# A boundary's instructions put in another order, and a last LayerNorm whose shift is summed by TensorE

## The chip, the cores and the metric

The kernel runs on one core of one Trainium2 chip. The core has five engines with queues of their own: TensorE (PE in the profile; PEld is its weight loads), VectorE (DVE), ScalarE (ACT), GpSimd (POOL) and SyncE (SP, which issues the transfers here). Each works through its queue in order, and semaphores tie the queues together. Data lie in HBM, in the SBUF (128 partitions) and in the PSUM, into which TensorE writes (8 banks of 512 fp32 per partition). The metric is the device time of one execution in microseconds.

## What is computed

One inference step of a two-layer decoder for a prompt of 256 tokens and for 8 samples of 4 tokens with the same weights, width 1024, all in fp32. Layer 0 mixes with a gated linear attention (GLA), layer 1 with dilated window attention over a shared key and value store. Each layer is FFN, mixer, FFN, and after each of these six sub-layers there is a LayerNorm:

```python
def modulate(x, shift, scale):
    return x * (1.0 + scale[:, None, :]) + shift[:, None, :]

def post_norm(x, y, gate, g, b):
    return layer_norm(ALPHA * x + (1.0 + gate[:, None, :]) * y, g, b)
...
        y = swiglu(modulate(x, sh1, sc1), p['w_ffn1_up'][l], p['w_ffn1_down'][l])
        x = post_norm(x, FFN_RES * y, g1, p['ln_g'][l, 0], p['ln_b'][l, 0])
        h = modulate(x, sh2, sc2)
        ...
        x = post_norm(x, y, g2, p['ln_g'][l, 1], p['ln_b'][l, 1])
        y = swiglu(modulate(x, sh3, sc3), p['w_ffn2_up'][l], p['w_ffn2_down'][l])
        x = post_norm(x, FFN_RES * y, g3, p['ln_g'][l, 2], p['ln_b'][l, 2])
```

The shifts, scales and gates come from products of a conditioning vector with `w_ada` (nine per layer, two more for keys and values).

## The kernel before, in words

**Layout.** All 288 tokens (256 of the prompt, 32 of the samples) stand in the free dimension, the width in 8 chunks of 128 partitions. `z` and `ax` hold the LayerNorm's input and the scaled residual, `xh` and `xl` the next sub-layer's input.

**Three products for one.** Each fp32 number is split into a high half, rounded to a faster type (fp32r), and a low half, the rest. `mm3` (from L529) makes high x high (L531), high weight x low input (L532) and low weight x high input (L533). The input's halves are xh and xl, the weight's are made by `split_part` (from L173): the high half by ScalarE (L177), the low half by VectorE (L179), a piece of 128 x 1024 at a time.

**The weight stream.** `Stream` loads all weights as one list of jobs (`job_list`), cut into pieces, through 11 raw buffers. A job is a weight ("w", split into one of 4 buffers for either half), raw data ("r"), or a step of the conditioning products ("ada": 16 TensorE matmuls for each, L450). `take` hands out the next weight and splits the one after it ahead; `more(n)` splits n more pieces; `fill` does the ada jobs that are next in the list. `weave` mixes two lists of jobs.

**Order.** The kernel's instructions are put in queue order by a list scheduler: by its own estimate of time, an engine that is free takes what is ready, first what the program wrote first. `pin(chain, ...)` makes an instruction follow the last one of the same chain ("act", "dve", "pe"). What is not pinned may be put into any gap that the scheduler sees.

**A boundary.** The LayerNorm between two sub-layers is prepared while the last products run (`Post.chunk`, `Post.stats`) and ended in `post_norm` (L771 to 801): `spread` brings 1/deviation to all partitions (L651), then for each of the 8 chunks VectorE subtracts the mean (`center`, L668), scales (L758, and for the samples L763 and L764), ScalarE rounds to xh (L760, L765), and VectorE makes xl (L767, L769). The xl of a chunk is issued after the first steps of the next chunk. At the third chunk one more weight piece is split (`S.more(1)`), both halves. All this is pinned. TensorE meanwhile begins the next sub-layer with `project_chunkwise`: the first two weights' four outputs, chunk by chunk (L549 and L551 for the first chunk, then L531 to L533).

**The residual.** `Post.residual` (from L670) forms ALPHA times the LayerNorm's output for the sub-layer after: per chunk one VectorE product (L676) and one addition of the bias on GpSimd (L678). It is a generator that yields after every second chunk. Its instructions are not pinned. The FFN draws it in its loop over the hidden dimension, two chunks per step; the GLA mixer draws all of it ahead of the keys' projection; the dilated mixer draws all of it after its first four outputs, ahead of their rotations. There are five boundaries, and so 40 of each of these two instructions.

**GLA and dilated mixer.** In the loop over `("wv", i)` (from L1159) the GLA mixer projects the values and between the projections prepares its decay levels on VectorE (`level`, four products and more for each level) and takes their products on TensorE. The dilated mixer rotates each projected query (`rotate`, L1288 to 1298): four copies by ScalarE (L1294), two products by VectorE (L1295) and GpSimd (L1296), a sum by VectorE (L1298). Its outputs stand in the four "pa" banks of the PSUM until L1294 and L1295 have read them.

**The last LayerNorm.** `Final` transposes each finished chunk of the sum back to tokens in partitions (L700, L701), takes statistics (L704, L707), multiplies by the gain (L711), and after the last chunk `finish` makes the output in six units (three token tiles, two halves of the width): a shift, gain x (-mean/deviation) + bias, and then y x (1/deviation) + shift (L736), which is stored (L738). Three units form the shift on VectorE (L730), three by ScalarE (L733) and GpSimd (L734):

```python
                if x in ON_DVE:
                    V.scalar_tensor_tensor(out=v, in0=gr[0:n, f], scalar=self.r[0:n, 1, t:t + 1], in1=br[0:n, f],
                                           op0=ALU.mult, op1=ALU.add)
                else:
                    A.mul(v, gr[0:n, f], self.r[0:n, 1, t:t + 1])
                    G.tensor_tensor(out=v, in0=v, in1=br[0:n, f], op=ALU.add)
                yv = self.y[0:n, t, f]
                V.scalar_tensor_tensor(out=yv, in0=yv, scalar=self.r[0:n, 0, t:t + 1], in1=v, op0=ALU.mult, op1=ALU.add)
```

## Time and profile before

| | |
|---|---|
| median of 3 runs | 1561.36 us (1559.15 to 1568.56) |
| the profiled execution | 1566.59 us |
| its span (first to last instruction) | 1564.5 us |
| TensorE busy | 1487.1 us, 95% |
| VectorE busy | 927.6 us, 59% |
| ScalarE busy | 715.7 us, 46% |
| GpSimd busy | 217.2 us, 14% |
| read from HBM | 332.36 MB, 218 GB/s over the span |

Times in the rows below are in microseconds from the span's start unless they are marked ns. A row of a timeline has the start, the duration, the engine, the line in the kernel, the operation, what it writes and reads, the sizes, how many such instructions were merged, and in brackets how long the engine had been idle and who ended that. Successive instructions overlap a little in such rows, so the distance between two starts tells more than a duration. A busy TensorE need not be at its full pace: a matmul that waits for its input can look busy.

### The profile page before, as it was taken

To read this page: it belongs to the slowest core of one execution; us is meant where nothing else is said; L and a number is where in the kernel's file an instruction comes from. 1 tells how busy PE (TensorE), PEld (TensorE's weight loads), DVE (VectorE), ACT (ScalarE), POOL (GpSimd) and SP (SyncE) were. 2 spreads that over 40 slices of the span, in tenths; PEclk is the share of its full clock that TensorE was granted. 3 is DMA by queue.
4 is the path that set the end of the run, shared out by engine and by line. 5 is a ranking of instruction groups with operands and counts; after the bars stand their busy time and mean duration, and the time that the engine had idled before them with its cause. 6 is when DMAs were issued, how large, how long until landed. Compare 5 with 4: busy or idle time off the path is not lost.

```text
span 1564.5 us, 31623 instructions
## 1 busy us (share of the span) xinstructions
PE 1487.1 (95%) x12706; PEld 1336.2 (85%) x12706; DVE 927.6 (59%) x2020; ACT 715.7 (46%) x1178; POOL 217.2 (14%) x312
## 2 busy tenths in 40 slices
PE   6999999999899999998999999999999989899996
PEld 4999998799778999998899999898766638899995
DVE  3644545596786444448745444675775667755455
ACT  2443434755744444346444433486543343444432
POOL 0000031201522000224100003232301002200001
PEclk8999999999999999999999999999998989999998
DMA  9977685636856767864566676767687997555520
GB/s 300 321 228 241 213 273 160 214 99 199 293 190 217 233 216 236 299 209 152 179 206 204 202 239 204 250 195 246 226 303 278 348 329 256 193 162 162 175 82 31
DMA packets 238420, 342.67 MB, mean 219 GB/s; under 512 B 12471, under 2 KB 201985, under 8 KB 238274
## 3 DMA queue, kind: packets, MB, share of 16 engines
q1 hardware_dynamic: 235810, 333.34, 64.7%
q0 software_dynamic: 2048, 7.14, 1.2%
q8 instruction: 99, 1.62, 0.4%
q14 instruction: 47, 0.39, 0.1%
q10 hardware_dynamic: 416, 0.17, 0.0%
HBM read 332.36 MB, written 8.26 MB: 218 GB/s over the span
## 4 chain that ended last, share of the span: by engine, by line
PE 83%; DVE 9%; ACT 3%; issue 2%; DMA 1%; POOL 0%; SPq 0%; DVEq 0%; ACTq 0%; POOLq 0%
PE pa L531 21%; PE pa L532 21%; PE pa L533 21%; PE pd L450 4%; PE pb L1381 4%; PE pa L1384 3%; PE pa L1381 2%; DVE lo L179 1%; PE pa L1042 1%; ACT pe L1407 1%; DVE xm L758 1%; DVE ax L676 1%; DMA xp<-in_x_prompt_dram 1%; ACT hi L177 0%; DVE lnacc L664 0%
## 5 line engine op out<-in xcount | busy, mean ns | idle before, releaser
L532 PE MATMUL pa<-xl,hi 128*128 128x288 f32 x1860 | 551.6, 298 | 6.8 <-DVE xl L769 6.8
L179 DVE TENSOR_TENSOR lo<-raw,hi 128x1024 fp32r<-128x1024 f32 x350 | 421.0, 1211 | 221.3 <-ACT hi L177 220.5
L533 PE MATMUL pa<-xh,lo 128*128 128x288 f32 x1860 | 547.6, 296 | 3.7 <-DVE lo L179 3.7
L531 PE MATMUL pa<-xh,hi 128*128 128x288 f32 x1860 | 543.5, 299 | 1.2 <-DVE lnsq L1295 0.8
L177 ACT ACTIVATE hi<-raw 128x1024 fp32r<-128x1024 f32 x350 | 358.7, 1035 | 260.6 <-PE pa L532 218.3
L532 PEld LDWEIGHTS pa<-xl,hi 128*128 128x128 f32 x1860 | 351.9, 189 | 14.0 <-DVE xl L769 9.4
L531 PEld LDWEIGHTS pa<-xh,hi 128*128 128x128 f32 x1860 | 347.9, 189 | 13.5 <-issue 10.0
L533 PEld LDWEIGHTS pa<-xh,lo 128*128 128x128 f32 x1860 | 351.7, 189 | 4.3 <-DVE lo L179 4.2
L531 PE MATMUL pa<-hh,hi 128*128 128x288 f32 x704 | 209.9, 298 | 0.0
L533 PE MATMUL pa<-hh,lo 128*128 128x288 f32 x704 | 208.1, 296 | 0.0
L532 PE MATMUL pa<-hl,hi 128*128 128x288 f32 x704 | 208.1, 296 | 0.0
L874 DVE TENSOR_TENSOR sa<-pa,sa 128x288 f32<-128x288 f32 x88 | 39.7, 454 | 179.9 <-PE pa L533 175.2
L531 PEld LDWEIGHTS pa<-hh,hi 128*128 128x128 f32 x704 | 132.6, 188 | 4.3 <-issue 2.9
L532 PEld LDWEIGHTS pa<-hl,hi 128*128 128x128 f32 x704 | 132.4, 188 | 0.2
L533 PEld LDWEIGHTS pa<-hh,lo 128*128 128x128 f32 x704 | 132.4, 188 | 0.1
L875 ACT ACTIVATE hh<-sa 128x288 fp32r<-128x288 f32 x88 | 38.7, 445 | 134.0 <-DVE sa L874 131.1
L873 ACT ACTIVATE sa<-pa 128x288 f32<-128x288 f32 x88 | 34.9, 401 | 93.6 <-PE pa L533 93.5
L450 PE MATMUL pd<-raw,cT 128*32 128x256 f32 x1008 | 73.3, 385 | 1.5 <-DMA raw<-in_w_ada_dram 1.4
L593 POOL TENSOR_TENSOR z<-z,lnpiv 128x288 f32<-128x288 f32 x6 | 4.7, 801 | 482.7 <-ACT lnpiv L588 482.7
L1384 PEld LDWEIGHTS pa<-ident,raw 128*128 128x128 f32 x448 | 49.7, 144 | 20.4 <-issue 9.4
L678 POOL TENSOR_SCALAR ax<-ax,lnba 128x288 f32<-128x288 f32 x40 | 54.9, 1376 | 71.3 <-DVE xm L764 69.4
L1384 PE MATMUL pa<-ident,raw 128*128 128x128 f32 x448 | 58.4, 282 | 5.4 <-ACT kt L1512 5.4
(380 smaller groups left out, 1761.4 us busy)
## 6 DMA issues: line engine op xcount, KB each, us to landing
raw<-in_w_ffn_up_dram SPq DMA_DIRECT2D x172, 512.0 KB, 4.8
raw<-in_w_ada_dram SPq DMA_DIRECT2D x110, 512.0 KB, 5.2
raw<-in_w_ffn_down_dram SPq DMA_DIRECT2D x80, 512.0 KB, 4.6
raw<-in_cache_k_dram SPq DMA_DIRECT2D x56, 512.0 KB, 6.7
raw<-in_cache_v_dram SPq DMA_DIRECT2D x56, 512.0 KB, 7.3
raw<-in_w_in_a_dram SPq DMA_DIRECT2D x24, 512.0 KB, 4.0
raw<-in_w_q_b_dram SPq DMA_DIRECT2D x24, 512.0 KB, 4.5
raw<-in_w_ada_dram SPq DMA_DIRECT2D x32, 256.0 KB, 5.8
```

What stands on the lines that cost most here:

```text
L177: self.pin("act", self.nc.scalar.activation(hv, src, AF.Copy))
L179: self.pin(low, eng.tensor_tensor(out=lo, in0=src, in1=hv.bitcast(F32), op=ALU.subtract))
L450: T.matmul(ps[32 * q:32 * q + 32, :], lhsT=cT[:, k, :], rhs=raw[kk][:, 256 * q:256 * q + 256], start=(k == 0), stop=(k == DC - 1), tile_po ...
L531: ins = [T.matmul(ps, lhsT=whi, rhs=xhi, start=first, stop=False), T.matmul(ps, lhsT=whi, rhs=xlo, start=False, stop=False), T.matmul(ps, ...
L532: T.matmul(ps, lhsT=whi, rhs=xlo, start=False, stop=False),
L533: T.matmul(ps, lhsT=wlo, rhs=xhi, start=False, stop=last)]
L678: G.tensor_scalar(out=ax[:, c, :], in0=ax[:, c, :], scalar1=bb_[:, c:c + 1], scalar2=None, op0=ALU.add)
L873: A.activation(sa, pa[:, 0:NT], AF.Silu)
L874: V.tensor_tensor(out=sa, in0=pu[:, 0:NT], in1=sa, op=ALU.mult)
L875: A.activation(hh[:, m, :], sa, AF.Copy)
L1381: pin("pe", T.matmul(*a, **k))
L1384: pin("pe", T.transpose(*a))
```

## The change

It has three parts.

1. `split_part` makes the high half at once and returns the low half as a second step. `post_norm` calls a new `begin` ahead of its loop over the chunks, which makes the high half of the next weight piece; the low half stays where it was, at the third chunk. The residual's VectorE products are pinned to the chain "dve". The GLA mixer draws its residual in the loop over `("wv", i)`, two chunks for each value weight.
2. In the list of jobs the ada jobs that were woven into the dilated mixer's query weights begin after six of them instead of four and end ahead of the last one.
3. In the last LayerNorm the shift of unit 0 stays on VectorE. For the five others it is summed in the PSUM by two products each: identity x bias, for four units written at the last chunk and for the fifth in `finish`, and diagonal matrix of -mean/deviation x gain. ScalarE makes the three diagonal matrices. GpSimd and the ScalarE products of 512 columns are gone from `finish`.

```diff
@@ Stream.part
-        self.split_part(self.split.setdefault(i, Weight()), self.jobs[i], self.raw.pop(x), f"{x}", low)
-        self.freed.add(x)
-        self.release()
-        return True
+        rest = self.split_part(self.split.setdefault(i, Weight()), self.jobs[i], self.raw.pop(x), f"{x}", low)
+
+        def end():
+            rest()
+            self.freed.add(x)
+            self.release()
+            return True
+
+        return end if low is None else end()
@@ Stream.split_part
         self.pin("act", self.nc.scalar.activation(hv, src, AF.Copy))
-        eng = self.nc.vector if low == "dve" else self.nc.gpsimd
-        self.pin(low, eng.tensor_tensor(out=lo, in0=src, in1=hv.bitcast(F32), op=ALU.subtract))
         w.append([y.rearrange("p k (m c) -> p m k c", c=min(P, cols)) for y in (hv, lo)])
+
+        def rest():
+            self.pin("dve", self.nc.vector.tensor_tensor(out=lo, in0=src, in1=hv.bitcast(F32), op=ALU.subtract))
+
+        return rest
@@ Stream
-    def more(self, n, low="dve"):
+    def more(self, n):
 
         self.pump()
-        while n and self.np < len(self.parts) and self.part(low):
+        while n and self.np < len(self.parts) and self.part():
             n -= 1
+
+    def begin(self):
+
+        self.pump()
+        end = self.part(None) if self.np < len(self.parts) else None
+        return end or (lambda: None)
@@ job_list
-    jobs += weave(wq, adas((1, 6))[x:] + adas((1, 7)), lead=4) + ca + wob + adas((1, 8))[2:]
+    jobs += weave(wq, adas((1, 6))[x:] + adas((1, 7)), lead=6, span=11) + ca + wob + adas((1, 8))[2:]
@@ Post.residual
-                V.scalar_tensor_tensor(out=ax[:, c, :], in0=z[:, c, :], scalar=ga[:, c:c + 1], in1=rstd, op0=ALU.mult,
-                                       op1=ALU.mult)
+                pin("dve", V.scalar_tensor_tensor(out=ax[:, c, :], in0=z[:, c, :], scalar=ga[:, c:c + 1], in1=rstd,
+                                                  op0=ALU.mult, op1=ALU.mult))
@@ Final.chunk
+            if c == DC - 1:
+
+                self.shift = {}
+                for x in range(1, 5):
+                    (t, h), n = divmod(x, 2), P if x < 4 else NS
+                    self.shift[x] = bankA()
+                    T.matmul(self.shift[x][0:n, :], lhsT=ident[0:n, 0:n], rhs=self.rows[0:n, 1, 512 * h:512 * h + 512],
+                             start=True, stop=False)
@@ Final.finish
+            diag = [self.fp.tile([P, P], F32, name=nm("dg"), tag=f"dg{t}") for t in range(3)]
+            for t in range(3):
+                A.mul(diag[t], ident, self.r[:, 1, t:t + 1])
+            self.shift[5] = bankB()
+            T.matmul(self.shift[5][0:NS, :], lhsT=ident[0:NS, 0:NS], rhs=br[0:NS, 512:1024], start=True, stop=False)
...
-                if x in ON_DVE:
+                if x == 0:
+                    v = ax.rearrange("p c t -> p (c t)")[0:n, 0:512]
                     V.scalar_tensor_tensor(out=v, in0=gr[0:n, f], scalar=self.r[0:n, 1, t:t + 1], in1=br[0:n, f],
                                            op0=ALU.mult, op1=ALU.add)
                 else:
-                    A.mul(v, gr[0:n, f], self.r[0:n, 1, t:t + 1])
-                    G.tensor_tensor(out=v, in0=v, in1=br[0:n, f], op=ALU.add)
+                    v = self.shift[x][0:n, :]
+                    T.matmul(v, lhsT=diag[t][0:n, 0:n], rhs=gr[0:n, f], start=False, stop=True)
@@ post_norm
+        low = S.begin()
         for c in range(DC):
...
             if c == 2:
-                S.more(1)
+                low()
@@ gla
-        for _ in residual:
-            pass
         qk("wk", kT, 1.0)
...
             w_ = S.take(("wv", i))
+            next(residual)
```

In the first group of the first FFN the low halves are still issued at once (`split_part(...)()`).

More of the change, by code (lines that the diff above doesn't have):

```diff
@@ L46 @@
 GAP = 0
-ON_DVE = (0, 1, 4)
 NQ = 72
@@ L723, in finish @@
             gr, br = self.rows[:, 0, :], self.rows[:, 1, :]
-            shift = ax.rearrange("p c t -> p (c t)")
-            units = [(t, h) for t in range(3) for h in range(2)]
-            for x, (t, h) in enumerate(units):
-                n, f = P if t < 2 else NS, slice(512 * h, 512 * h + 512)
-                v = shift[0:n, 512 * (x % 4):512 * (x % 4) + 512]
-                if x in ON_DVE:
+            diag = [self.fp.tile([P, P], F32, name=nm("dg"), tag=f"dg{t}") for t in range(3)]
[3 more added lines that the diff above has]
+            T.matmul(self.shift[5][0:NS, :], lhsT=ident[0:NS, 0:NS], rhs=br[0:NS, 512:1024], start=True, stop=False)
+            for x in range(6):
+                (t, h), n = divmod(x, 2), P if x < 4 else NS
+                f = slice(512 * h, 512 * h + 512)
+                if x == 0:
+                    v = ax.rearrange("p c t -> p (c t)")[0:n, 0:512]
                     V.scalar_tensor_tensor(out=v, in0=gr[0:n, f], scalar=self.r[0:n, 1, t:t + 1], in1=br[0:n, f],
@@ L848, in first_group @@
             for i in range(2):
-                S.split_part(w[i], jfirst[i], wfirst[i][:, k0:k0 + 4, :], f"f{i}{k0}")
+                S.split_part(w[i], jfirst[i], wfirst[i][:, k0:k0 + 4, :], f"f{i}{k0}")()
             if k0 == 0:
```

## The prediction

> **What bounds the kernel now.** I read the page's span and chain first, then the answers for single lines, then the timelines of the five boundaries and of the end. The page's chain (shares of the span by line), and the residual's products (L676: count, then ns min/median/max, first and last start):
>
> ```profile
> span 1564.5 us, 31623 instructions
> ...
> PE pa L531 21%; PE pa L532 21%; PE pa L533 21%; PE pd L450 4%; PE pb L1381 4%; PE pa L1384 3%; PE pa L1381 2%; DVE lo L179 1%; PE pa L1042 1%; ACT pe L1407 1%; DVE xm L758 1%; DVE ax L676 1%; DMA xp<-in_x_prompt_dram 1%; ACT hi L177 0%; DVE lnacc L664 0%
> ```
> ```profile
> L676 DVE SCALAR_TENSOR_TENSOR ax<-z,lnga,lnacc x40: 509/514/521, 271.2 to 1343.1; 128x288 f32<-128x288 f32 x40
> ```
>
> TensorE carries the chain; VectorE takes it only in short stretches, and L676 (the residual of the next sub-layer, which nobody needs soon) is among them. Those stretches are the five LayerNorm boundaries. TensorE there does 96 products (four outputs, eight chunks, three products) and follows VectorE chunk by chunk. First and last product of each boundary, in order of time (start, duration), with a piece of gapless pace in the third; the last row is one ada step:
>
> ```profile
> 270.55 0.40 PE L549 MATMUL pa<-xh,hi 128*128 128x288 f32 x1
> ...
> 289.67 0.29 PE L533 MATMUL pa<-xh,lo 128*128 128x288 f32 x1
> ...
> 466.33 0.40 PE L549 MATMUL pa<-xh,hi 128*128 128x288 f32 x1
> ...
> 486.25 0.29 PE L533 MATMUL pa<-xh,lo 128*128 128x288 f32 x1
> ...
> 708.87 0.40 PE L549 MATMUL pa<-kh,hi 128*128 128x288 f32 x1
> ...
> 726.85 0.29 PE L533 MATMUL pa<-kh,lo 128*128 128x288 f32 x1
> ...
> 727.25 0.29 PE L533 MATMUL pa<-kh,lo 128*128 128x288 f32 x1
> ...
> 1005.47 0.40 PE L549 MATMUL pa<-xh,hi 128*128 128x288 f32 x1
> ...
> 1025.05 0.29 PE L533 MATMUL pa<-xh,lo 128*128 128x288 f32 x1
> ...
> 1328.49 0.40 PE L549 MATMUL pa<-xh,hi 128*128 128x288 f32 x1
> ...
> 1346.88 0.29 PE L533 MATMUL pa<-xh,lo 128*128 128x288 f32 x1
> ```
> ```profile
> 63.12 1.00 PE pd L450 x16
> ```
>
> The pace is (727.25 - 726.85) / 3 = 0.133 us, so 96 products are 12.8 us of work. The five stretches last 19.1, 19.9, 18.4, 19.6 and 18.4 us. In the first, second and fourth the scheduler slipped in some 32, 32 and 46 ada matmuls (1.00 / 16 = 0.0625 us each: 2.0, 2.0, 2.9 us). What is lost is then 4.3, 5.1, 5.6, 3.9 and 5.6 us: 24.5 us in all.
>
> **The change, boundary part.** What VectorE does in the last boundary (its next rows repeat the cycle), and ScalarE beside it:
>
> ```profile
> 1332.91 1.23 DVE L179 TENSOR_TENSOR lo<-raw,hi 128x1024 fp32r<-128x1024 f32 x1
> ...
> 1336.06 0.45 DVE L668 TENSOR_TENSOR z<-z,pb 128x288 f32<-128x288 f32 x1
> ...
> 1337.05 0.51 DVE L676 SCALAR_TENSOR_TENSOR ax<-z,lnga,lnacc 128x288 f32<-128x288 f32 x1
> 1337.47 0.19 DVE L764 TENSOR_TENSOR xm<-xm,affb 128x32 f32<-128x32 f32 x1
> ...
> 1338.08 0.45 DVE L668 TENSOR_TENSOR z<-z,pb 128x288 f32<-128x288 f32 x1
> ```
> ```profile
> 1327.25 0.51 ACT L760 ACTIVATE xh<-xm,affb 128x256 fp32r<-128x256 f32 x1 [2.42 <-DVE xm L758]
> ...
> 1331.84 1.04 ACT L177 ACTIVATE hi<-raw 128x1024 fp32r<-128x1024 f32 x1
> ```
>
> One chunk costs VectorE 1338.08 - 1336.06 = 2.02 us, TensorE 12 x 0.133 = 1.6 us: VectorE sets the pace. Pinning the residual behind the chain takes out a slot of 1337.47 - 1337.05 = 0.42 us per chunk. Some 0.1 us may stay, since the add of L764 waits for the product before it, so the new cycle is 1.6 to 1.7 us, about TensorE's own. Three of the eight slots lie ahead of the weight's low half (L179), five behind. The high half (L177, 1.04 us) moves ahead of the chunks, into ScalarE's idle 2.42 us before the first L760: it costs nothing there, and L179, which starts at 1332.91 just after L177 ends at 1332.88, no longer waits. Were that weight piece not loaded, all of ScalarE's chain would wait behind it; L177 ran in the old place without a wait on a transfer, so I book nothing, with a loss as the rival below shows.
>
> Following the chain for the last boundary with 1.7 us a chunk: the third chunk's xl comes about 1.8 us earlier (three slots of 0.42, some wait for L177), the five later cycles give 5 x 0.31 more, so 96 products end 3.1 us earlier and last 15.3 instead of 18.4. The same for the third boundary (no ada inside it): 3.1. In the first and second the ada matmuls now find about half of the gaps: 2.0 us of them still have to be done, so I take 2.3 and 2.8. Sum for four boundaries: -11.3. The ends: 0 if TensorE takes other waits instead, and the whole loss of these four, -20.6. I stand nearer the middle because TensorE's first three chunks still wait (the low half of 1.1 us lies before the third).
>
> **Where the residual goes.** In three boundaries it goes into an FFN loop, two products per step, where TensorE is gapless: nothing. In the GLA mixer it goes into the wv loop. Windows there (span, then busy PE, PEld, DVE, ACT, POOL):
>
> ```profile
> 312.00:342.00 30.00, 30.00 (x257) 28.37 (x256) 27.61 (x49) 16.02 (x28) 0.00 (x0) 1.00 0.37 112
> 342.00:372.00 30.00, 30.00 (x278) 26.16 (x276) 28.36 (x57) 14.04 (x24) 1.94 (x1) 1.00 0.54 176
> ```
>
> VectorE is idle for only 2.4 + 1.6 = 4.0 of 60 us, and 8 x 0.42 = 3.4 us are put in. Some idle time cannot be used (waits on other engines). Bounds 0 and +3.4; I take +1.
>
> In the dilated mixer the residual stays where the code had it, but pinned: behind the low halves, ahead of the first rotations. TensorE waits for these, since the four products hold all four pa banks. ScalarE, VectorE and TensorE there, and GpSimd's two kinds of work:
>
> ```profile
> 1022.44 1.99 ACT L177 ACTIVATE hi<-raw 128x1024 fp32r<-128x1024 f32 x2
> 1024.46 3.30 ACT L1294 ACTIVATE xm<-pa 32x288 f32<-32x288 f32 x8
> ```
> ```profile
> 1023.52 2.36 DVE L179 TENSOR_TENSOR lo<-raw,hi 128x1024 fp32r<-128x1024 f32 x2 [0.38 <-ACT hi L177]
> 1026.13 0.46 DVE L1295 TENSOR_TENSOR lnsq<-pa,ropeq 128x288 f32<-128x288 f32 x1 [0.25 <-ACT xm L1294]
> 1027.01 0.42 DVE L1298 TENSOR_TENSOR z<-lnsq,xm 128x256 f32<-128x256 f32 x1 [0.42 <-POOL xm L1296]
> ```
> ```profile
> 1026.64 0.40 PE L531 MATMUL pa<-xh,hi 128*128 128x288 f32 x1 [0.76 <-DVE lnsq L1295]
> ```
> ```profile
> 1026.18 0.79 POOL L1296 TENSOR_TENSOR xm<-xm,ropeq 128x288 f32<-128x288 f32 x1 [3.25 <-ACT xm L1294]
> ```
> ```profile
> L678 POOL TENSOR_SCALAR ax<-ax,lnba x40: 997/1380/1729, 271.8 to 1343.7; 128x288 f32<-128x288 f32 x40
> ```
>
> VectorE's chain ends some 3.5 us earlier, so the two low halves end at 1025.8 - 3.5 = 1022.3; then eight residual products, 3.4 us, to 1025.7; only then L1295, and TensorE goes on at 1026.3 instead of 1026.6. The gain of this boundary is so used up. Of the 46 ada matmuls only some 16 still fit (with lead 6 their transfers come later), 1.9 us to be done afterwards. Each residual product is followed by L678 on GpSimd, 0.997 to 1.729 us each, and all eight stand ahead of the rotation's product there (L1296): at 1.1 us they end at 1022.8 + 8.8 = 1031.6, the third bank is free after L1296 (0.79), L1298 (0.42), four copies (3.30 / 2 = 1.65) and L1295 (0.46), at 1034.9, and TensorE wants it at 1026.3 + 48 x 0.133 = 1032.7. That is 2.2 us of stall, partly filled with ada. I take -0.3 + 1.9 + 2.2 - 0.8 = +3. The ends: at 1.729 us each, +8; if a rotation slips in ahead of the residual, -1.5. The order of the weight stream (lead 6, span 11) adds no work and is priced inside this term. The other edits (the low half as a second step called at once, `more` without its parameter) issue the same instructions in the same order: nothing.
>
> **The last LayerNorm.** Rows of the end (in the second fence ns min/median/max; the last two show plain fp32 products, two records each):
>
> ```profile
> 1549.65 0.28 PE L701 MATMUL pb<-ident,z 128*32 128x128 f32 x1
> ```
> ```profile
> L736 DVE SCALAR_TENSOR_TENSOR yt<-yt,rn,ax x6: 732/740/1752, 1553.6 to 1560.6; 128x512 f32<-128x512 f32 x4, 32x512 f32<-32x512 f32 x2
> ```
> ```profile
> 1552.23 1.42 DVE L730 SCALAR_TENSOR_TENSOR ax<-rows,rn 128x512 f32<-128x512 f32 x2
> 1553.10 3.34 POOL L734 TENSOR_TENSOR ax<-ax,rows 128x512 f32<-128x512 f32 x2 [207.68 <-ACT ax L733]
> ...
> 1559.90 1.39 DVE L736 SCALAR_TENSOR_TENSOR yt<-yt,rn,ax 32x512 f32<-32x512 f32 x2
> ```
> ```profile
> 294.40 3.45 PE L984 MATMUL pa<-wg,ga 17*128 17x512 f32 x6 [0.19 <-ACT ga L1005]
> ...
> 389.16 3.46 PE pa L1207 x16
> ```
>
> VectorE ends at 1561.29. L736 takes 0.74 us alone and 1.75 beside GpSimd's L734, which goes away. VectorE's own new work from 1552.23 is 0.71 + 6 x 0.74 = 5.2 us, to 1557.4. But TensorE gets ten fp32 products of 512 columns: L1207 gives 3.46 / 16 x 2 x 2 = 0.865 us each (256 columns a record), L984 3.45 / 3 = 1.15. From the last transpose (1549.93) ten of them end at 1558.6 or 1561.4, less 0.65 us if one runs while TensorE waits for the last z; one L736 follows. So VectorE ends near 1559.3 (gain 2.0), at the ends 1557.4 (-3.9) and 1562.2 (+0.9). The diagonal matrices (ScalarE, 128 columns) are ready before TensorE gets to them. I take -2, by L1207, whose records follow without a wait.
>
> **The sum.** -11.3 + 3 + 1 - 2 = -9.3: span 1555.2. The profiled execution took 1566.59 us, 5 more than the median of 1561.36 shown; the same gain from the median gives 1552.
>
> **Rivals.** (1) *All gaps close*: boundaries -14.5, no loss in the dilated mixer (-1.5), wv free, end -2.4: 1543. For it: VectorE's cycle falls to TensorE's. Against it: the queue order at the rotations. (2) *Hidden anyway*: only recorded TensorE idle comes back. The waits of TensorE:
>
> ```profile
> PE pa L532 <- DVE xl L769: 6.8, 10, 2.2
> ```
>
> Two thirds of that, 4.5, less 4 for wv and dilated, and 2 at the end: -2.5, 1559. For it: ada work moved out has to be done later. (3) *The dilated start costs its 8*: -4.3, 1557. (4) *Slower*: GpSimd's eight L678, now inside the wv loop, hold VectorE up there as L734 does L736 (about 1.0 us each, up to 1.7). VectorE then has 3.4 + 8 x 1.7 = 17 us more against 4.0 idle, and TensorE waits for the decay levels that VectorE prepares: +13 instead of +1, so 1564; it decides from 1.4 us each on (3.4 + 8 x 1.4 - 4.0 = 10.6, more than the 10.3 gained elsewhere). Against it: L676 itself, two inputs in SBUF and run beside L678, took 0.509 to 0.521 us in all forty. The Trainium skill, in SBUF — State Buffer, section Who interferes with whom, says that a VectorE instruction with two SBUF inputs and a GpSimd one that reads SBUF shut each other out for a whole instruction. That would be this rival in full; L736 beside L734 agrees with it and L676 beside L678 does not, so it gets a small chance.
>
> **How the numbers follow.** A measurement of this kernel tells about 1% (15.6 us) from no change. Forecast 0.55, rival 1 0.12, rival 2 0.15, rival 3 0.08, rival 4 0.10. Faster by over 1% (below 1545.8) only in rival 1, nearly all of it: 0.11. Slower by over 1% (above 1577) needs rival 4 and the dilated loss together: 0.03. Within 1%: 0.86. The range leaves out half of rival 1 and most of rival 4: 1545 to 1562; the forecast's own is 1547 to 1557.
>
> **What would show it.** L676 behind the last xl of each boundary and 96 products in about 15.3 us: boundary right; over 17.5: wrong. L177 before the first L760. In the dilated mixer L676 between L179 and L1295, and eight L678 ahead of L1296. TensorE idle against VectorE's levels in the wv loop: rival 4. At the end L736 at 0.74 us and waiting on TensorE; if it does not wait, the fp32 price was too high. A wait of L177 on a transfer at a boundary would break the cover I gave it.

## The result, and the profile after

The changed kernel took 1552.04 us (median of 7 runs, 1549.38 to 1559.25) beside 1561.36 (7 runs, 1559.15 to 1568.56): a ratio of 0.9940, 95% interval 0.9925 to 0.9955, so 7 to 12 us less. Run again beside the experiments it gave 0.9922 (0.9908 to 0.9936). The profiled execution took 1554.06 us with a span of 1552.1, 12.4 below the span of before; part of these 12.4 is chance, as shown below. Of the chain, VectorE's share fell from 9% to 6%, and that of transfers rose from 1% to 4%.

The chain by engine before; then the page's span and chain after, as in the prediction (shares of the span, first by engine, then by line; lines have moved down by 4 to 25):

```profile
PE 83%; DVE 9%; ACT 3%; issue 2%; DMA 1%; POOL 0%; SPq 0%; DVEq 0%; ACTq 0%; POOLq 0%
```
```profile
span 1552.1 us, 31653 instructions
...
PE 82%; DVE 6%; DMA 4%; ACT 3%; issue 2%; POOL 1%; SPq 0%; ACTq 0%; POOLq 0%; DVEq 0%
PE pa L544 21%; PE pa L545 21%; PE pa L546 21%; PE pd L463 4%; PE pb L1406 4%; PE pa L1409 3%; DMA raw<-in_w_ada_dram 2%; PE pa L1406 2%; PE pa L1066 1%; ACT pe L1432 1%; DMA w<-in_w_ffn_up_dram 1%; DVE lo L185 1%; DMA qT<-in_w_ada_dram 1%; ACT xm L1319 1%; DVE xm L783 1%
```

The residual's product (now L689, `ax`) and ScalarE's high half (now L181, `hi`) are no longer among the lines of this chain that the page lists; a new entry is the transfer of ada blocks, `raw<-in_w_ada_dram`, 2%. First and last of the 96 products at the four boundaries that were meant to gain (start, duration), to be laid beside the prediction's rows:

```profile
271.57 0.40 PE L562 MATMUL pa<-xh,hi 128*128 128x288 f32 x1
...
288.12 0.29 PE L546 MATMUL pa<-xh,lo 128*128 128x288 f32 x1
...
462.51 0.40 PE L562 MATMUL pa<-xh,hi 128*128 128x288 f32 x1
...
478.35 0.29 PE L546 MATMUL pa<-xh,lo 128*128 128x288 f32 x1
...
702.17 0.40 PE L562 MATMUL pa<-kh,hi 128*128 128x288 f32 x1
...
717.27 0.29 PE L546 MATMUL pa<-kh,lo 128*128 128x288 f32 x1
...
1321.87 0.40 PE L562 MATMUL pa<-xh,hi 128*128 128x288 f32 x1
...
1336.97 0.29 PE L546 MATMUL pa<-xh,lo 128*128 128x288 f32 x1
```

They last 16.6, 15.8, 15.1 and 15.1 us, where they lasted 19.1, 19.9, 18.4 and 18.4. (In the second, 14 of the 32 ada matmuls now stand behind the 96th product; up to the next product it takes 17.1 us, where it took 20.1.) ScalarE and VectorE at the last boundary:

```profile
1318.11 1.04 ACT L181 ACTIVATE hi<-raw 128x1024 fp32r<-128x1024 f32 x1
...
1320.62 0.51 ACT L785 ACTIVATE xh<-xm,affb 128x256 fp32r<-128x256 f32 x1 [1.48 <-DVE xm L783]
```
```profile
1324.54 1.22 DVE L185 TENSOR_TENSOR lo<-raw,hi 128x1024 fp32r<-128x1024 f32 x1
...
1330.80 0.45 DVE L681 TENSOR_TENSOR z<-z,pb 128x288 f32<-128x288 f32 x1
...
1332.50 0.45 DVE L681 TENSOR_TENSOR z<-z,pb 128x288 f32<-128x288 f32 x1
...
1335.11 2.36 DVE L185 TENSOR_TENSOR lo<-raw,hi 128x1024 fp32r<-128x1024 f32 x2 [0.32 <-ACT hi L181]
1337.39 0.51 DVE L689 SCALAR_TENSOR_TENSOR ax<-z,lnga,lnacc 128x288 f32<-128x288 f32 x1
```

The high half runs in ScalarE's idle time ahead of the first chunk, and waits for no transfer. The low half (L185) follows its predecessor without a wait. The cycle from chunk to chunk is 1332.50 - 1330.80 = 1.70 us where it was 2.02, and the first residual product stands behind everything.

### Where the 12.4 us of the two profiles come from

Both kernels issue the same 8280 products of the kind `mm3` in nearly the same order (28 change places, within two boundaries), so the start of the n-th of them can be compared. The table cuts the span at such products. A boundary reaches from its first product to the first after its 96; the dilated start reaches from the boundary's first product to the first of the last query output; the cache stage from there to the out-projection. "Control" is the changed kernel's second profile (the experiment after_again).

| stretch, us | before | after | control |
|---|---|---|---|
| up to the first boundary | 270.6 | 271.6 | 269.8 |
| four boundaries | 78.16 | 66.10 | 66.12 |
| GLA mixer up to its out-projection | 136.6 | 135.6 | 135.6 |
| GLA out-projection | 40.1 | 38.7 | 40.2 |
| FFN loops and shared keys (three stretches) | 699.99 | 700.28 | 700.32 |
| dilated boundary and query products | 91.5 | 96.8 | 95.3 |
| cache stage | 191.1 | 189.1 | 185.8 |
| dilated out-projection | 40.5 | 40.5 | 39.6 |
| last product to the end | 16.2 | 13.5 | 13.4 |

The four boundaries give 12.1, to 0.02 us alike in both profiles; the end gives 2.7. The dilated start loses 3.8 to 5.3. The rest moves by chance: a kernel whose GLA mixer, out-projection and cache stage are those of before (the experiment tail_only) had 135.1, 40.1 and 187.5 there, with 79.3 in the four boundaries and 92.4 in the dilated start.

Most of that chance is the granted clock. In every profile it falls to 0.50 now and then, for 3.4 us or a multiple, and TensorE's products then start 0.24 us apart, not 0.133. The GLA out-projection took 38.6 to 38.7 us in the four profiles without such a drop, 40.0 to 40.2 in the seven with one, 41.4 to 41.6 in the three with two: by these, a drop costs about 1.4 us there. The 12.1 of the boundaries stands: the kernel before had one drop there, in the third, which took 19.85 us with it and 19.84 without one in tail_only, and the changed kernel had none. The dilated start had no drop in the kernel before and one in both profiles of the changed kernel, so by the same estimate some 1.4 of its loss may be the clock's. The control right after TensorE goes on there, and the experiment threaded at the same place (span, busy PE, PEld, DVE, ACT, POOL, then the clock, the DMA share and GB/s):

```profile
1017.80:1021.30 3.50, 3.50 (x17) 3.50 (x16) 3.30 (x5) 3.22 (x8) 3.50 (x3) 0.51 0.86 262
```
```profile
1018.50:1022.00 3.50, 3.50 (x30) 3.43 (x27) 2.59 (x7) 3.39 (x8) 0.99 (x2) 1.00 0.75 252
```

TensorE did 17 matmuls in the first and 30 in the second.

### The profile page after: what moved, and what is told of

Read it like the earlier page. It is cut to its first block, busy times and chain, and to the rows that moved or that the text cites. A ratio compares the mean times of both kernels' runs of the same rounds, so it can differ in the third digit from the quotient of the medians.

```text
span 1552.1 us, 31653 instructions
## 1 busy us (share of the span) xinstructions
PE 1490.8 (96%) x12726; PEld 1334.2 (86%) x12726; DVE 924.9 (60%) x2018; ACT 713.3 (46%) x1180; POOL 212.3 (14%) x309
## 4 chain that ended last, share of the span: by engine, by line
PE 82%; DVE 6%; DMA 4%; ACT 3%; issue 2%; POOL 1%; SPq 0%; ACTq 0%; POOLq 0%; DVEq 0%
PE pa L544 21%; PE pa L545 21%; PE pa L546 21%; PE pd L463 4%; PE pb L1406 4%; PE pa L1409 3%; DMA raw<-in_w_ada_dram 2%; PE pa L1406 2%; PE pa L1066 1%; ACT pe L1432 1%; DMA w<-in_w_ffn_up_dram 1%; DVE lo L185 1%; DMA qT<-in_w_ada_dram 1%; ACT xm L1319 1%; DVE xm L783 1%
## 5 line engine op out<-in xcount | busy, mean ns | idle before, releaser
L185 DVE TENSOR_TENSOR lo<-raw,hi 128x1024 fp32r<-128x1024 f32 x350 | 421.4, 1212 | 219.2 <-ACT hi L181 212.7
L181 ACT ACTIVATE hi<-raw 128x1024 fp32r<-128x1024 f32 x350 | 358.4, 1035 | 259.5 <-PE pa L545 213.0
L544 PEld LDWEIGHTS pa<-xh,hi 128*128 128x128 f32 x1860 | 347.6, 189 | 14.6 <-issue 9.5
L900 DVE TENSOR_TENSOR sa<-pa,sa 128x288 f32<-128x288 f32 x88 | 39.6, 454 | 169.0 <-PE pa L546 165.4
L901 ACT ACTIVATE hh<-sa 128x288 fp32r<-128x288 f32 x88 | 38.7, 445 | 135.8 <-DVE sa L900 133.1
L691 POOL TENSOR_SCALAR ax<-ax,lnba 128x288 f32<-128x288 f32 x40 | 58.2, 1464 | 202.8 <-DVE ax L689 202.5
L899 ACT ACTIVATE sa<-pa 128x288 f32<-128x288 f32 x88 | 34.9, 401 | 92.5 <-PE pa L546 92.4
L1319 ACT ACTIVATE xm<-pa 32x288 f32<-32x288 f32 x128 | 51.5, 402 | 20.2 <-issue 6.4
```

The costliest lines, as they stand in the source:

```text
L181: self.pin("act", self.nc.scalar.activation(hv, src, AF.Copy))
L185: self.pin("dve", self.nc.vector.tensor_tensor(out=lo, in0=src, in1=hv.bitcast(F32), op=ALU.subtract))
L544: ins = [T.matmul(ps, lhsT=whi, rhs=xhi, start=first, stop=False), T.matmul(ps, lhsT=whi, rhs=xlo, start=False, stop=False), T.matmul(ps, ...
L691: G.tensor_scalar(out=ax[:, c, :], in0=ax[:, c, :], scalar1=bb_[:, c:c + 1], scalar2=None, op0=ALU.add)
L900: V.tensor_tensor(out=sa, in0=pu[:, 0:NT], in1=sa, op=ALU.mult)
L901: A.activation(hh[:, m, :], sa, AF.Copy)
```

## The experiments

Each ratio is to the kernel before on the same chip (median 1561.1 to 1562.3 us there); 0.001 is 1.6 us.

### The last LayerNorm alone (tail_only)

The kernel before, with `Final.chunk` and `Final.finish` of the changed one:

```diff
-                if x in ON_DVE:
...
-                    G.tensor_tensor(out=v, in0=v, in1=br[0:n, f], op=ALU.add)
+                    v = self.shift[x][0:n, :]
+                    T.matmul(v, lhsT=diag[t][0:n, 0:n], rhs=gr[0:n, f], start=False, stop=True)
```

> The kernel before with the last LayerNorm of the change alone. Theory (the end is an item of its own: VectorE loses the two slow L736 and GpSimd's adds, and then waits on TensorE): 2.5 us below the kernel before, 2.0 to 3.0, so a ratio near 0.998, and the last VectorE product some 1.5 to 2.5 us earlier after the last z. Rival (the end only looks shorter because work ahead of it moved): no difference, within 0.5 us, and the same distance from the last z to the last instruction as before.

Measured: 0.9984 (0.9974 to 0.9994), 2.5 us less. From the last product to the end of the span it took 13.5 us where the kernel before took 16.2. The end is an item of its own, of the expected size; the rival is out.

### The high half back in its old place (no_begin)

```diff
-        low = S.begin()
...
             if c == 2:
-                low()
+                S.more(1)
```

> The changed kernel with the high half of the weight piece back in its old place, after the third chunk. Theory (the pinned residual is most of the gain, the early high half only takes a short wait out of VectorE's order): about 0.5 us lost at each of four boundaries, 2 us in all over the changed kernel; the 96 products take about 0.5 us longer each. Rival A (the early high half is what shortens the boundaries): 6 to 10 us lost. Rival B (it does nothing): within 0.5 us of the changed kernel.

Measured: 0.9964 (0.9952 to 0.9975), 4 to 7 us slower than the changed kernel by its two ratios. The four boundaries take 70.5 us, 4.4 more. ScalarE and VectorE at the last boundary:

```profile
1325.23 1.04 ACT L181 ACTIVATE hi<-raw 128x1024 fp32r<-128x1024 f32 x1
```
```profile
1326.30 1.22 DVE L185 TENSOR_TENSOR lo<-raw,hi 128x1024 fp32r<-128x1024 f32 x1 [0.47 <-ACT hi L181]
```

Here the high half stands after the third chunk on ScalarE, and VectorE is idle for 0.47 us before the low half, behind which its next five chunks are pinned. Counted from the boundary's first product, the low half begins 0.9 us later than in the changed kernel, at each of the four. The loss is 0.9 us at this boundary (16.83 us, not 15.94) and 1.95 at the third, where the clock dropped to 0.50 for 3.4 us and in the changed kernel did not; without that excess of 1.0 the four lose 3.4. Either is more than the 2 of the theory and less than rival A's. So the early high half is about a third of the boundaries' gain.

### The residual's product not pinned (no_pin)

```diff
-                pin("dve", V.scalar_tensor_tensor(out=ax[:, c, :], in0=z[:, c, :], scalar=ga[:, c:c + 1], in1=rstd,
-                                                  op0=ALU.mult, op1=ALU.mult))
+                V.scalar_tensor_tensor(out=ax[:, c, :], in0=z[:, c, :], scalar=ga[:, c:c + 1], in1=rstd,
+                                       op0=ALU.mult, op1=ALU.mult)
```

> The changed kernel with the residual's product not pinned into VectorE's order. Theory (the pin moves the residual out of the chunks): the product comes back between the chunks, 8 times 0.42 us less what TensorE covers, so some 2.5 us lost at each of four boundaries, 8 to 11 us in all; in the dilated mixer the eight products move ahead too and the third bank waits less for GpSimd, up to 3 us back: 6 to 10 us lost in the sum. Rival (the early high half sets the order): within 1 us of the changed kernel.

Measured: 0.9968 (0.9949 to 0.9987), 4 to 7 us slower than the changed kernel. Its eight runs spread from 1552.3 to 1562.9, and the profile is of the fastest. VectorE at the last boundary:

```profile
1326.52 0.45 DVE L681 TENSOR_TENSOR z<-z,pb 128x288 f32<-128x288 f32 x1
...
1327.50 0.51 DVE L689 SCALAR_TENSOR_TENSOR ax<-z,lnga,lnacc 128x288 f32<-128x288 f32 x1
...
1328.53 0.45 DVE L681 TENSOR_TENSOR z<-z,pb 128x288 f32<-128x288 f32 x1
```

The residual is back in every cycle, which is 2.01 us long. The four boundaries take 74.5 us, 8.4 more than in the changed kernel; the dilated start takes 93.6, 1.8 to 3.3 less, and has no drop of the clock. Pin and early high half give 8.4 and 3.4 to 4.4, together about the 12.1 that the boundaries gained.

### GpSimd's additions later, twice (adds_later, adds_pinned)

In the changed kernel's profile the dilated start reads so (TensorE, VectorE, GpSimd):

```profile
1014.91 0.29 PE L546 MATMUL pa<-xh,lo 128*128 128x288 f32 x1
...
1017.89 0.40 PE L544 MATMUL pa<-xh,hi 128*128 128x288 f32 x1
...
1028.95 0.40 PE L544 MATMUL pa<-xh,hi 128*128 128x288 f32 x1 [1.25 <-DVE lnsq L1320]
```
```profile
1012.05 3.52 DVE L689 SCALAR_TENSOR_TENSOR ax<-z,lnga,lnacc 128x288 f32<-128x288 f32 x8
1015.73 0.46 DVE L1320 TENSOR_TENSOR lnsq<-pa,ropeq 128x288 f32<-128x288 f32 x1 [0.15 <-ACT xm L1319]
...
1027.43 1.00 DVE L1323 TENSOR_TENSOR z<-lnsq,xm 128x256 f32<-128x256 f32 x1 [4.63 <-POOL xm L1321]
```
```profile
1019.29 7.33 POOL L691 TENSOR_SCALAR ax<-ax,lnba 128x288 f32<-128x288 f32 x6
1026.59 1.55 POOL L1321 TENSOR_TENSOR xm<-xm,ropeq 128x288 f32<-128x288 f32 x2
```

TensorE goes on 2.98 us after its 96th product (1.59 before the change); the two waits recorded there, 0.88 and 0.60 us, are for ada transfers. Later it waits 1.25 us for a bank whose rotation waits for GpSimd, where six of the residual's additions, 7.33 us, stand ahead of the third rotation's product. The two waits that follow (0.33 and 0.88 us) are for low halves of weight pieces, which stand behind the rotations in VectorE's queue.

The first edit only wrote the additions later:

```diff
                     rotate(p_, tab, q_out(2 * hq + m, g))
+                    if adds:
+                        adds.popleft()()
```

> The changed kernel with GpSimd's eight additions of the dilated mixer's residual put behind later rotations, one each; the same work in another place of its queue. Theory (six additions ahead of the third rotation's product hold TensorE's bank): TensorE's waits at the third, fourth and fifth bank, 1.55, 0.62 and 1.18 us, go; 3 us below the changed kernel, 2 to 3.5. Rival (the loss there is ada work that comes later, in TensorE's own time): the waits go but the time stays, within 0.7 us.

Measured: 0.9931 (0.9919 to 0.9943). It shows nothing for or against: nothing on GpSimd was pinned, so the scheduler put the same six additions ahead of the third rotation again, and TensorE had the same waits. The second edit pins GpSimd's order:

```diff
+        x = G.tensor_tensor(out=sw, in0=sw, in1=tab[:, 1, :], op=ALU.mult)
+        if adds is not None:
+            pin("pool", x)
+            if adds:
+                pin("pool", adds.popleft()())
```

> The changed kernel with GpSimd's order in the dilated mixer fixed: the rotations' products in turn, and the residual's eight additions one behind each of the fifth to twelfth. (In the run before, the additions were written later but came out in the same place of GpSimd's queue, so it tested nothing.) Theory (six additions ahead of the third rotation hold TensorE's banks): TensorE's waits of 1.55, 0.62 and 1.18 us in the query products go; the dilated start and the query products together, 96.8 us in the changed kernel's profile, take 93.5; some 3 us below the changed kernel beside it. Rival (the loss is ada work that comes later): the waits go, other waits or ada matmuls take their place, and the stretch stays within 1 us of 96.8.

Measured: 0.9926 (0.9907 to 0.9944). The waits among the query products are gone; the stretch takes 94.0 us, 1.3 below the control beside it, not 3. What is left of TensorE's waits from 1008 us to 1037 us:

```profile
1012.66 0.64 PE L463 MATMUL pd<-raw,cT 128*32 128x256 f32 x8 [0.85 <-DMA raw<-in_w_ada_dram]
1014.62 0.64 PE L463 MATMUL pd<-raw,cT 128*32 128x256 f32 x8 [1.32 <-DMA raw<-in_w_ada_dram]
1016.03 0.61 PE L544 MATMUL pa<-xh,hi 128*128 128x288 f32 x1 [0.77 <-DVE lnsq L1327]
```

All of them lie between the 96th product (1011.52) and the first query product. GpSimd's queue is one part of the loss; the restart, 4.5 us after the 96th product, is another.

### The weight stream in its old order (old_stream, both_pinned), and the control (after_again)

```diff
-    jobs += weave(wq, adas((1, 6))[x:] + adas((1, 7)), lead=6, span=11) + ca + wob + adas((1, 8))[2:]
+    jobs += weave(wq, adas((1, 6))[x:] + adas((1, 7)), lead=4) + ca + wob + adas((1, 8))[2:]
```

> The changed kernel with the weight stream of the dilated mixer in its old order. Theory GpSimd (its queue makes the loss, the stream is free): the waits of 1.55, 0.62 and 1.18 us stay, the time is within 1 us of the changed kernel's. Theory ada (sixteen ada matmuls come late and TensorE waits for their transfers at the boundary): the wait of 2.5 us among the 96 products goes and the ada matmuls come back into the gaps: 2 us below the changed kernel.

> Both edits: GpSimd's order fixed and the weight stream in its old order. If the two losses are separate they add: 3 + 2 = 5 us below the changed kernel, the stretch back at 91.5 or below, the kernel before's. If GpSimd's queue is all, as the first alone. If both only move waits, within 1 us of the changed kernel.

> The changed kernel once more, as the control beside the three. Every theory: a ratio of 0.993 to 0.995 to the kernel before, and the same waits of 1.55, 0.62 and 1.18 us in the query products. The cache stage that follows, which took 191.1 us in the kernel before and 189.1 in the changed one, tells by its spread over these four (none of the edits touches it) how much of a single profile is chance: if it spreads over 2 us or more, its 2 us in favour of the change were none of the change's.

Measured: 0.9919 (0.9902 to 0.9936), 0.9931 (0.9916 to 0.9947) and 0.9922 (0.9908 to 0.9936); the stretch 95.8, 96.8 and 95.3 us. The control first. It went on at 1016.82, 4.4 us after its 96th product (VectorE, then TensorE):

```profile
1011.84 4.55 DVE L689 SCALAR_TENSOR_TENSOR ax<-z,lnga,lnacc 128x288 f32<-128x288 f32 x8
1016.32 0.81 DVE L1320 TENSOR_TENSOR lnsq<-pa,ropeq 128x288 f32<-128x288 f32 x2
```
```profile
1012.43 0.29 PE L546 MATMUL pa<-xh,lo 128*128 128x288 f32 x1
...
1016.82 0.40 PE L544 MATMUL pa<-xh,hi 128*128 128x288 f32 x1 [1.49 <-DVE lnsq L1320]
```

In this execution TensorE waited less for ada transfers, the 96 products took 17.2 us and not 19.4, and now the eight residual products ahead of L1320 were what it waited for. They took 4.55 us, not 3.52, since GpSimd was at work beside them: the first rotation's product on GpSimd ran from 1013.29 to 1014.29, and the residual product that began within it took 1.06 us. In the first profile they were hidden behind ScalarE's copies, because TensorE was late. Two expectations of the control failed: its ratio lies just below the 0.993 to 0.995, and of the three waits in the query products one was there (0.84 us).

The old stream does take the transfers' waits out of the 96 products (they took 17.4 us with 32 ada matmuls among them; in the first profile of the changed kernel 19.4 with 16), and then a wait follows on the next ada block, 3.61 us in old_stream and 5.02 in both_pinned. In old_stream:

```profile
1017.49 1.06 PE L463 MATMUL pd<-raw,cT 128*32 128x256 f32 x2 [3.61 <-DMA raw<-in_w_ada_dram]
```

In old_stream the waits among the query products are gone, though GpSimd has six additions ahead of the third rotation as before: TensorE came later. So neither theory of these runs held: the waits moved, and the two edits did not add. The stream's new order is worth nothing here that these profiles could show, either way.

The cache stage, which no edit touches, took 187 to 188.5 us in three of these profiles and 186 in the control. Its spread over all fourteen profiles of this study is 185.7 to 191.1 us, and it goes with the granted clock there: 0.991 in the four shortest (185.7 to 185.8 us), 0.952 in the longest. Windows there of the kernel before and of the control (columns as above):

```profile
1145.00:1193.00 48.00, 42.87 (x504) 28.34 (x502) 29.47 (x116) 17.79 (x39) 5.45 (x29) 0.89 0.83 308
```
```profile
1138.00:1185.00 47.00, 41.87 (x541) 27.87 (x530) 31.49 (x125) 18.89 (x42) 5.48 (x29) 1.00 0.83 314
```

Over the whole span, too, the profile of before had the lowest mean clock of the fourteen (0.980), and the control the highest (0.994). The 2.0 us that the first pair of profiles shows there are none of the change's.

### The residual threaded between the rotations (threaded)

Each product behind one rotation's first VectorE instruction, each addition behind a rotation's product on GpSimd, in the order in which the rotations overwrite `z`:

```diff
+        y = V.tensor_tensor(out=t1, in0=ps[:, 0:NT], in1=tab[:, 0, :], op=ALU.mult)
+        if muls:
+            pin("dve", y)
+            muls.popleft()()
...
+        order = (0, 3, 1, 4, 2, 5, 6, 7)
+        muls = deque(lambda c=c: mul(c) for c in order)
+        adds = deque(lambda c=c: add(c) for c in order)
```

> The changed kernel with the dilated mixer's residual threaded between the rotations: each of the eight products behind one rotation's first VectorE instruction, each of the eight additions on GpSimd behind a rotation's product from the fifth on. Theory (eight products, 3.5 to 4.6 us, ahead of the first rotation hold TensorE, which in the control's profile went on 4.4 us after its 96th product, in the kernel before 1.6): it goes on within 2 us of the 96th product, and the stretch of the boundary and the query products, 95.3 in the control and 94.0 with GpSimd's order alone, takes 91 to 92; some 4 us below the changed kernel. Rival (it is the transfers of ada blocks that hold TensorE there, freed by the ring of weight buffers): a wait of 3 us or more on such a transfer takes the place of the bank's, and the stretch stays at 94 or more.

Measured: 0.9922 (0.9910 to 0.9934), and the stretch takes 92.0 us: 3.4 below the control's, 0.5 above that of before. TensorE, VectorE and GpSimd at the restart:

```profile
1017.02 0.29 PE L546 MATMUL pa<-xh,lo 128*128 128x288 f32 x1
1018.00 0.64 PE L463 MATMUL pd<-raw,cT 128*32 128x256 f32 x8 [0.69 <-DMA raw<-in_w_ada_dram]
1018.57 0.40 PE L544 MATMUL pa<-xh,hi 128*128 128x288 f32 x1
```
```profile
1017.84 0.46 DVE L1330 TENSOR_TENSOR lnsq<-pa,ropeq 128x288 f32<-128x288 f32 x1 [0.98 <-ACT xm L1329]
1018.21 0.79 DVE L689 SCALAR_TENSOR_TENSOR ax<-z,lnga,lnacc 128x288 f32<-128x288 f32 x1
```
```profile
1017.88 0.80 POOL L1334 TENSOR_TENSOR xm<-xm,ropeq 128x288 f32<-128x288 f32 x1 [24.77 <-ACT xm L1329]
```

TensorE goes on 1.55 us after its 96th product, as before the change and 2.8 sooner than in the control: at the restart the order of the residual and the rotations makes the loss. The rival as stated (a wait of 3 us or more on a transfer) is out; such waits are 1.1 us among the 96 products and 0.69 here. The query products did not gain (73.6 us; 73.8 in the control, 70.3 before). The control had a drop of the clock among them and this profile none, so by the estimate above some 1.4 of the 3.4 us may be the clock's. Over all the experiments, the six profiles in which TensorE meets the rotations in the changed kernel's order (the changed kernel twice, no_begin, adds_later, wv_triple and tail_two) show 95.3 to 96.8 us for this stretch, with one drop each; threaded and the experiment best show 92.0 and 93.1, the kernel before and tail_only 91.5 and 92.4, all four without a drop. Whether the order brings the drop about isn't shown. The whole time does not show the gain: 3.4 us are 0.2% and the interval is as wide; in this profile the GLA mixer and its out-projection, which the edit doesn't touch, were 3.3 us longer than in the control, with two more drops of the clock.

### GpSimd three times as busy in the value loop (wv_triple)

```diff
+                if (l, s) == (0, 0):
+                    for _ in range(2):
+                        G.tensor_scalar(out=ax[:, c, :], in0=ax[:, c, :], scalar1=1.0, scalar2=None, op0=ALU.mult)
```

> The changed kernel with two more passes of GpSimd over each chunk of the residual in the value loop of the GLA mixer (a multiplication by one): 24 GpSimd passes there in place of 8. Theory (VectorE loses its own time only, GpSimd beside it costs next to nothing): the stretch from the first boundary's end to the out-projection, 135.6 us, grows by less than 1 us, and VectorE's products there stay below 0.55 us. The prediction's fourth rival (GpSimd shuts VectorE out for whole instructions, 1.0 to 1.7 us each): sixteen more such stops, VectorE 16 us or more later, the stretch longer by 8 us or more.

Measured: 0.9917 (0.9904 to 0.9930); the GLA stretch 136.1 us, 0.5 longer. The windows of the prediction, for the changed kernel and for this one:

```profile
312.00:342.00 30.00, 30.00 (x257) 27.84 (x256) 29.31 (x56) 15.29 (x29) 10.14 (x6) 1.00 0.36 106
342.00:372.00 30.00, 30.00 (x283) 26.44 (x285) 28.75 (x56) 16.40 (x24) 4.43 (x3) 1.00 0.61 194
```
```profile
312.00:342.00 30.00, 30.00 (x256) 28.00 (x256) 29.66 (x56) 14.20 (x27) 22.79 (x18) 1.00 0.35 98
342.00:372.00 30.00, 30.00 (x286) 25.84 (x285) 29.54 (x56) 17.29 (x26) 9.01 (x7) 1.00 0.60 192
```

GpSimd's busy time doubles (14.6 to 31.8 us), VectorE's grows by 1.1, TensorE stays at 30.00 of 30. The fourth rival falls. Two of the eight products were 0.67 us and not 0.51 (expected: below 0.55), so VectorE does lose something beside GpSimd, but next to nothing.

### Two shifts on VectorE (tail_two)

```diff
-                if x == 0:
-                    v = ax.rearrange("p c t -> p (c t)")[0:n, 0:512]
+                if x < 2:
+                    v = ax.rearrange("p c t -> p (c t)")[0:n, 512 * x:512 * x + 512]
```

> The changed kernel with two of the six shifts of the last LayerNorm on VectorE and four on TensorE, in place of one and five. Theory (at the end VectorE waits for TensorE's fp32 products, 0.43 us a record, four records less): the last L761 ends some 0.7 us earlier after the last z, and the time is 0.7 us below the changed kernel's, too little for the runs to show but not for the profile. Rival (VectorE is the bound there): 0.7 us longer, one more L755.

Measured: 0.9920 (0.9904 to 0.9935); from the last product to the end 12.2 us where all kernels with the end of the change had 13.4 to 13.5. VectorE and TensorE in the changed kernel:

```profile
1543.24 0.75 DVE L761 SCALAR_TENSOR_TENSOR yt<-yt,rn,ax 128x512 f32<-128x512 f32 x1
1544.79 2.46 DVE L761 SCALAR_TENSOR_TENSOR yt<-yt,rn,pa 128x512 f32<-128x512 f32 x3 [0.80 <-PE pa L759]
...
1548.34 0.73 DVE L761 SCALAR_TENSOR_TENSOR yt<-yt,rn,pb 32x512 f32<-32x512 f32 x1
```
```profile
1543.63 3.81 PE L759 MATMUL pa<-rows,dg 128*128 128x512 f32 x8
1547.28 1.02 PE L759 MATMUL pb<-rows,dg 32*32 32x512 f32 x2
```

L761 takes 0.75 us, waits 0.80 for TensorE's first product, and the last one follows TensorE's last record. TensorE is the bound at the end, and four records fewer give 1.3 us, more than the 0.7 expected.

### Both edits that held (best)

`threaded` and `tail_two` in one kernel, so their two diffs.

> The changed kernel with the two edits that its stages bore out: the dilated mixer's residual threaded between the rotations (3.4 us less in that stretch's profile than the control), and two shifts of the last LayerNorm on VectorE (1.3 us less from the last FFN product to the end). They lie in different stages, so they should add: the boundary and the query products at 92 us, the end at 12.1 us, 4.7 us below the changed kernel, a ratio near 0.990 to the kernel before. Rival (the stretch's gain is given back in the cache stage, which follows the transfers): the two stages as short as in their own runs, but a ratio of 0.992 to 0.994, the changed kernel's.

Measured: 1548.03 us, 0.9910 (0.9893 to 0.9927). The end takes 12.2 us, the dilated stretch 93.1. Against the kernel before it is the lowest ratio of the study, but its interval overlaps the control's and that of wv_triple (0.9917), which adds work and changes no order: that it beats the changed kernel is not shown by the runs, only by its two stages, the dilated one with the reserve above. In its profile the cache stage took 190.2 us at a granted clock of 0.96 there.

## Why the prediction was right

The forecast of 1552 and its range held. Point by point:

- **Boundaries** (-11.3): -12.1. The residual stands behind the last xl, the two that have no ada inside took 15.1 us where 15.3 was forecast, and no L181 waited for a transfer. The mechanism held, with one share too small: the wait of the low half for the high half, priced in half a sentence as "some wait" (1.8 less three slots of 0.42, so 0.5 at each boundary, 2.2 in all), is worth 3.4 to 4.4 us of it (no_begin), the residual's slots 8.4 (no_pin). The sum has a slip as well: 1.8 and 5 x 0.31 make 3.35 a boundary, not the 3.1 it goes on with; the two without ada gained 3.3.
- **FFN loops** (0): 0.3 us in 700.
- **GLA value loop** (+1): nothing above chance (135.6 us; 136.6 and 135.1 in the two profiles with the old loop). TensorE stayed busy there, even with three times the GpSimd work.
- **Dilated start** (+3): +5.3 in the first profile, +3.8 in the second: the right sign and place, mis-sized; some 1.4 of either may be the drop of the clock, for which the sum had no term. The step "all eight stand ahead of the rotation's product there" failed in its detail: two rotations slipped in and six additions stood ahead of the third. The step "-0.3" for the restart was the larger miss: counted from the boundary's first product, TensorE went on after 22.4 us, in the control after 21.5, where it had taken 21.2. In the first profile the recorded waits ahead of that are for ada transfers (2.2 us among the 96 products, 1.5 behind them); in the control 1.4 and 1.3 are, and 1.5 are for the first rotation behind the eight residual products. These were costed at 0.42 each; in the control they took 4.55 / 8 = 0.57 on average, and threaded takes that wait away. The "+1.9" was for 30 ada matmuls that no longer fit, and 16 did stand among the 96 as forecast; the waits for their transfers had no term beyond the 1.4 that the kernel before had too. The query products, +3.3 by the other terms (1.9 + 2.2 - 0.8), took 4.1 and 3.5 us longer.
- **Last LayerNorm** (-2): -2.7, alone -2.5. L736 (now L761) fell to 0.75 us and waits on TensorE, as said; eight fp32 records took (1547.28 - 1543.63) / 8 = 0.46 us each, near the 0.43 that L1207 gave.
- **The sum** (-9.3): -9.3 in the medians; in the control's runs -11.2 by the medians, -12.2 by the ratio. The stages that the change touches give -12.1 + 4.6 - 2.7 = -10.2, the 4.6 being the mean of the two profiles. The agreement to the last digit is luck; within 3 us it is not.

Of the rivals, the first (all gaps close) was wrong at the rotations; the second (hidden anyway) at the boundaries, where more than TensorE's recorded idle time came back; the third had its place right and its price too high; the fourth was tested and is out.

What stays open: how much of the dilated loss is the ada transfers in a given execution, and how much the clock. Two profiles of one kernel differ there by 1.5 us, and the wait changes place from run to run. Open, too, is the clock's share in the whole gain: the 51 runs of the kernel before beside the experiments had a mean clock of 0.984, the changed kernel's 0.987 and, in the control, 0.990. Inside either group of runs 0.01 of the clock goes with about 5 us, so some 2 us may be the clock's, and nothing here shows whether the change raises it.

## What to carry to other kernels

Pinning side work behind a chain pays where the next stage is gapless, and costs where the next stage opens with work on the same engine: there, thread it between that work, one piece each. An edit that only writes an instruction later in the program is no experiment where a scheduler orders the queues; look at the queue's order first. And compare stages, cut at the same instruction in both traces, before a total is explained: 3 to 5 us of this total came and went with the granted clock.

## What the runs showed of the hardware

- A VectorE product with two SBUF inputs (L689) took 0.51 us alone, and 0.79 when it began beside GpSimd's L1334, which reads two SBUF inputs (rows of threaded): it ended 0.32 us after that instruction did. In the fourteen profiles 21 such products began while a two-input instruction of GpSimd ran and took 0.69 to 1.10 us, and each ended 0.31 to 0.32 us after it. Two others, in tail_two, took 0.51, and there GpSimd's instruction took 1.99 us in place of 0.80. The Trainium skill (SBUF — State Buffer, section Who interferes with whom) says that such a pair excludes one another for a whole instruction. These rows agree with it.
- Beside GpSimd's one-input additions it is otherwise: of 103 such products that began while an addition alone ran, 79 took no longer than alone and 24 took 0.67 to 0.76 us, and in the value loop the sixteen added GpSimd passes cost VectorE 1.1 us of busy time in all, far below an exclusion per instruction.
- The granted clock fell to 0.50 for 3.4 us at a time, at places that differ between executions of the same work. It moved the cache stage by up to 5 us of 190, and the GLA out-projection by 1.4 us for each drop.
